# Grouping the score matmuls of an attention job, and sorting the experts ahead of the first expert group

## The chip, the cores and the metric

The kernel runs on 1 core of one Trainium2 chip. The metric is the device time in microseconds (us), the median of 3 runs. A profile of one more execution comes with it: every instruction of the five engines with its start, the DMA queues, and the clock that TensorE was granted (1.00 is 2.4 GHz, 0.50 is 1.2 GHz).

## The reference

One block of a hybrid model on 512 tokens of width 1024. Two branches, differential attention and a chunked state space scan (SSD), are merged through gates and an output projection. Then a hierarchical mixture of experts follows. What the change touches, cut to its core:

```python
# attention: 8 heads, each with two components c of width 64, causal, blocks of 128 queries
scores = einsum('bqhcd,bkhcd->bhcqk', q[:, q_lo:q_hi], k[:, :q_hi]) * scale
probs = softmax(where(causal, scores, -inf), axis=-1)
weights = probs[:, :, 0] - lam * probs[:, :, 1]
outs.append(einsum('bhqk,bkhe->bqhe', weights, v[:, :q_hi]))

# experts: 8 groups of 8, a token takes the 2 best experts of its best group
eid = g_sel * 8 + top_k(e_logits[g_sel], 2)
hid = silu(x @ w_gate[e]) * (x @ w_up[e])      # 64 experts, hidden width 512
out[token] += weight * (hid @ w_down[e])       # summed over the token's 2 experts
```

Everything is float32.

## The kernel before

**Two parts.** Up to the output projection the work is planned by a small scheduler in the program, `Flow`. Jobs with an engine, a cost, a priority and tokens for the buffers are sorted into one fixed order per engine before anything runs. The big weight matrices are cut into units of 512 columns (`unit`, matmuls on line 243). Each is split into a high and a low part, and each product is three matmuls. These unit matmuls have the lowest priority and fill TensorE between the jobs of the attention and of the SSD scan. The expert part behind it is written out by hand, in a loop over groups of experts.

**A score job (`att`, `sc`, lines 664 to 673).** For a head, a block of 128 queries and a component c there is a job of three matmuls into one PSUM bank. The first, line 669, takes all 128 rows of the array: 64 rows with the high part of the scaled queries and 64 with their low part, against the high part of the keys, which stands there twice (`qa`, `kk`). The second, line 671, takes 64 rows: the high part of the queries against the low part of the keys (`kl`), in rows 0 to 63 for c = 0 and 64 to 127 for c = 1. The third, line 673, adds the causal mask through an identity in bf16. The number of keys is 128, 256, 384 or 512. Behind the job VectorE takes the negative row maximum (line 676), ScalarE the exponential with its row sum (680), VectorE joins both components (685 to 687), TensorE transposes the result (692), ScalarE copies it (696), TensorE multiplies it with the values (701) and VectorE scales (709). PSUM has 5 banks for this side work (`side()`).

**The experts.** All 64 experts are computed, in groups whose tokens fill the 128 columns of the stationary operand: a pair has 64 places for each expert, a four 32. Tokens beyond these places go through a loop at the end, which `overflow_tables` prepares. So the experts with most tokens should stand in pairs. `order_tables` (line 1588) sorts them by their counts and permutes the routing tables `ptab` with it. The first `NS` = 4 experts keep their places, so that their weights can be loaded before anything is known of the counts. For the others the queue on SyncE reads the expert's number from the table `perm` and loads from a dynamic address (`source`, line 1216).

An expert has 6 transfers of 1 MB: 4 of gate and up, 2 of down. They are issued in the order of the groups (`tiles`). 15 buffers hold them. `done` and `fill` issue the next ones as matmuls free buffers; in the queue a transfer whose buffer is not yet free holds up all behind it. In the order before, six pairs come first and 13 fours behind them.

**A group (the loop from line 1763).** Gate and up product (`gate_up`, matmuls on line 1701, 8 steps over the width, two of which free one buffer of each expert), SiLU on ScalarE and VectorE (1705 to 1707), the hidden rows transposed (`hidden_t`, 1713), the down product (1724), scaled rows (`weighted`), and one group later the sum into the tokens' rows (`combine`, 1740 to 1746). Selection matrices for two groups are made at a time (`onehot`), and one `gather` (1440 and 1441) collects the tokens' rows for both. `group_slots` (1682 to 1690) transposes a selection matrix and takes the routing weights. In the first group the last six steps of the gather stand between the steps of gate-and-up (`pre`); behind gate-and-up come `group_slots`, `order_tables`, `hidden_t`, `overflow_tables`, the second `group_slots` and the down product, in this order on every engine.

Of the kernel before, what the change touches and what calls it, by code (L numbers as in the profile page):

```python
# [13 lines left out]
AF = mybir.ActivationFunctionType  # L14
# [10 lines left out]
class Flow:  # L25
# [32 lines left out]
    def put(self, j):  # L58
        if j["e"] == "N":
            self.zero.append(j)  # L60
        else:
            self.ready[j["e"]].append(j)
# [56 lines left out]
def block_kernel(ctx: ExitStack, tc: tile.TileContext, I, out):  # L119
    nc = tc.nc  # L120
    V, A, G, T = nc.vector, nc.scalar, nc.gpsimd, nc.tensor
# [6 lines left out]
    def side():  # L128
        return sps.tile([128, 512], F32, name="s")
# [12 lines left out]
    J = fl.job  # L142
# [11 lines left out]
    def cv(n):  # L154
        return 0.07 + n * 0.00104
# [105 lines left out]
    ident = cst([128, 128], "ident")  # L261
    V.tensor_scalar(ident, iot, 0.0, None, op0=OP.is_equal)
    identb = cst([128, 128], "identb", BF)
# [3 lines left out]
    maskq = cst([128, 128], "maskq", BF)  # L267
# [94 lines left out]
    j = sqj[0]  # L362
# [204 lines left out]
    def tl(name, shape, bufs, dt=F32):  # L567
        return pools["at"].tile(shape, dt, name=name, bufs=bufs)
# [5 lines left out]
    def ev_qk(p):  # L574
        S_ = {}
# [81 lines left out]
        def att(qb, hh):  # L657
            kl = (qb + 1) * 128
            qs = slice(qb * 128, kl)
            t = {}  # L660
            h = 2 * p + hh
            vc = slice((h % 4) * 128, (h % 4) * 128 + 128)

            def sc(c):
                if c == 0:
                    t["nm"] = tl("nm", [128, 8], 12)
                t["s", c] = side()
                r = slice(64 * c, 64 * c + 64)
                T.matmul(t["s", c][:, :kl], lhsT=S_["qa"][:, c, hh, qs], rhs=S_["kk"][:, c, hh, :kl],
                         start=True, stop=False)  # L670
                T.matmul(t["s", c][:, :kl], lhsT=S_["qa"][r, c, hh, qs], rhs=S_["kl"][r, hh, :kl],
                         start=False, stop=False)
                T.matmul(t["s", c][:, qs], lhsT=identb, rhs=maskq, start=False, stop=True)

            def mx(c):
                V.tensor_reduce(t["nm"][:, c:c + 1], t["s", c][:, :kl], axis=AX.X, op=OP.max, negate=True)

            def ex(c):
                t["p", c] = tl(("p1", "p2")[c], [128, S], (3, 2)[c])
                A.activation(t["p", c][:, :kl], t["s", c][:, :kl], AF.Exp, bias=t["nm"][:, c:c + 1],  # L680
                             accum_out=t["nm"][:, 2 + c:3 + c])

            def un():
                nm, p1, p2 = t["nm"], t["p", 0], t["p", 1]
                V.reciprocal(nm[:, 4:6], nm[:, 2:4])
                V.tensor_scalar(nm[:, 6:7], nm[:, 2:3], nm[:, 5:6], nlam, op0=OP.mult, op1=OP.mult)
                V.scalar_tensor_tensor(p1[:, :kl], p2[:, :kl], nm[:, 6:7], p1[:, :kl], op0=OP.mult, op1=OP.add)

            def tr():
                t["tp"] = side()  # L690
                for kb in range(qb + 1):
                    T.transpose(t["tp"][:, kb * 128:kb * 128 + 128], t["p", 0][:, kb * 128:kb * 128 + 128], ident)

            def ut():
                t["ut"] = tl("ut", [128, NCH, 128], 2)
                A.activation(t["ut"][:, :qb + 1], t["tp"].rearrange("p (b n) -> p b n", b=4)[:, :qb + 1], AF.Copy)

            def av():
                t["av"] = side()
                for kb in range(qb + 1):  # L700
                    T.matmul(t["av"][:, :128], lhsT=t["ut"][:, kb], rhs=vt[p // 2][:, kb, vc],
                             start=(kb == 0), stop=(kb == qb))

            def ev():
                if qb == 0:
                    asb[hh] = tl("asb", [128, NCH, 128], 4)
                    if hh == 0:
                        st[0] = tl("ast", [128, 3, 2, NCH], 2)
                V.tensor_scalar(asb[hh][:, qb], t["av"][:, :128], t["nm"][:, 4:5], None, op0=OP.mult)

            def eq():
                A.activation(t["av"][:, :128], asb[hh][:, qb], AF.Square, accum_out=st[0][:, 0, hh, qb:qb + 1])

            es = []
            for c in range(2):
                j = J("P", 0.06 + max(0.22, kl * 0.00084), lambda c=c: sc(c), list(trj), prio=2.5, acq=["s"])
                scj[p].append(j)
                j = J("V", cv(kl), lambda c=c: mx(c), [j], prio=1.5)
                es.append(J("A", ca(kl), lambda c=c: ex(c), [j], prio=1.5, acq=[("p1", "p2")[c]], rel=["s"]))
            j = J("V", 0.5 + cv(kl), un, es + [lamj], prio=1.5, rel=["p2"])  # L720
            j = J("P", 0.107 * (qb + 1), tr, [j], prio=2.4, acq=["s"])
            j = J("A", ca(kl), ut, [j], prio=1.4, acq=["ut"], rel=["s", "p1"])
            j = J("P", 0.218 * (qb + 1), av, [j] + vj[p // 2], prio=2.3, acq=["s"], rel=["ut"])
            avj[p].append(j)
            j = J("V", 0.27, ev, [j], prio=1.3, acq=["asb"] if qb == 0 else [])
            eqs.append(J("A", 0.23, eq, [j], prio=1.3, rel=["s"]))
            if qb == 3 and hh == 1:
                finish()
# [391 lines left out]
    def mt(tag, shape, name, dt=F32):  # L1120
        if tag is None:
            return pools["mp"].tile(shape, dt, name=name)
        return pools["mp"].tile(shape, dt, name=name, tag=tag, bufs=tags[tag])
# [72 lines left out]

    NS, NW = 4, 12
    groups = ([list(range(i, i + 2)) for i in range(0, NW, 2)] + [list(range(i, i + 4)) for i in range(NW, 64, 4)])  # L1200
    NG = len(groups)
    tiles = []
    for g_ in groups:
# [383 lines left out]

    def order_tables():

        ox = mt("y", [128, 1024], "ox")  # L1590
        key, i64, w1, lt_ = (ox[:, i * E:i * E + E] for i in range(4))
        bd = ox[:, 512:640]
        kc, pc, cc_ = (ox[:, i:i + 1] for i in (640, 641, 642))
        tT = mt("y", [128, 4, 128], "tT")
        V.tensor_scalar(key, R["cnt"], 64.0, None, op0=OP.mult)
        V.tensor_tensor(key, key, iota1, op=OP.subtract)
        V.tensor_scalar(key[:, :NS], iota1[:, :NS], -1.0, 1.0e6, op0=OP.mult, op1=OP.add)
        V.tensor_tensor(i64, ident[:, :E], ident[:, E:], op=OP.add)
        V.tensor_tensor(w1, key, i64, op=OP.mult)
        V.tensor_reduce(kc, w1, axis=AX.X, op=OP.add)  # L1600
        V.tensor_scalar(lt_, key, kc, None, op0=OP.is_gt)
        V.tensor_reduce(pc, lt_, axis=AX.X, op=OP.add)
        V.tensor_scalar(pc, pc, 1.0, None, op0=OP.add)
        V.memset(bd, 0.0)
        for i in range(2):
            r = slice(64 * i, 64 * i + 64)
            V.tensor_scalar(bd[r, 64 * i:64 * i + 64], iota1[r], pc[r], None, op0=OP.is_equal)
        ps = side()
        T.matmul(ps[:1, :E], lhsT=pidx[:E], rhs=bd[:E, :E], start=True, stop=True)
        V.tensor_copy(R["perm"], ps[:1, :E])  # L1610
        V.tensor_tensor(w1, R["cnt"], i64, op=OP.mult)
        V.tensor_reduce(cc_, w1, axis=AX.X, op=OP.add)
        ps = side()
        T.matmul(ps[:, :E], lhsT=cc_[:E].to_broadcast([E, 128]), rhs=bd[:E, :E], start=True, stop=True)
        V.tensor_copy(R["cnt"], ps[:, :E])
        ps = side()
        for i in range(4):
            T.transpose(ps[:, 128 * i:128 * i + 128], ptab[:, i], ident)
        A.activation(tT, ps.rearrange("p (i n) -> p i n", i=4), AF.Copy)
        ps = side()  # L1620
        for i in range(4):
            T.matmul(ps[:, 128 * i:128 * i + 128], lhsT=tT[:, i], rhs=bd, start=True, stop=True)
        A.activation(ptab, ps.rearrange("p (i n) -> p i n", i=4), AF.Copy)

    def overflow_tables():

# [35 lines left out]
    def gather1(P, xt, k):  # L1662
        ps = side()
        gather_mm(P, 256, ps[:, :256], k, range(NCH))
        A.activation(xt[:, k], ps[:, :256], AF.Copy)
# [94 lines left out]

    xt, P = xt[0], R["P0"]
    pend = None
    for gi, g_ in enumerate(groups):
        n = len(g_)
        w = 128 // n
# [5 lines left out]
                fill()  # L1771

        def pre(k):
            if gi == 0 and 1 <= k < 7:
                gather1(P, xt, k + 1)
            elif last and k == 4:
                combine(*pend)

# [8 lines left out]
        hh = gate_up(xt[:, :, o:o + 128], n, w, wk("gu"), done, pre)  # L1787
        if gi == 0:
            ps_ = group_slots(P, 0)
            order_tables()  # L1790
        elif not last:
            combine(*pend)
        if last:
            keep_warm(8)
        ht = hidden_t(hh, 128)
        if gi == 0:
            overflow_tables()
        pt, sl = ps_
        if gi % 2 == 0:
# [172 lines left out]
```

## Time and profile before

| | us |
|---|---|
| runs | 1858.61, 1858.28, 1858.57; median 1858.57 |
| profiled execution, its own time | 1860.44 |
| its span, first to last instruction | 1858.6 |
| TensorE busy | 1636.6 (88%) |
| VectorE busy | 785.3 (42%) |
| ScalarE busy | 416.3 (22%) |
| GpSimd busy | 316.9 (17%) |
| bytes read | 471.56 MB, 255 GB/s over the span |

The engines are called PE (TensorE; PEld its weight loads), DVE (VectorE), ACT (ScalarE), POOL (GpSimd) and SP (SyncE, which issues the transfers). A busy share is an average over stages that have different limits, so the stretches below are cut where the limit changes. The profile's starts of matmuls are measured and their ends modelled: what one costs in a sequence is read from start to start.

### The profile page before, as it was taken

The page shows a single profiled execution, that of the slowest core. Times are in us where ns is not written, and L with a number is a line of the kernel's source. Part 1 is how long each engine was busy: PE and PEld are TensorE (multiplying, and loading weights), DVE is VectorE, ACT ScalarE, POOL GpSimd, SP SyncE. Part 2 cuts the span into 40 slices and gives each one's busy share as a digit, 9 for nine tenths or more (in the row PEclk, how much of TensorE's full clock was granted, in tenths as well). Part 3 has the DMA queues.
Part 4 walks back from the last instruction along what each step waited for, and adds up shares of the span by engine and source line. Part 5 has one row for each costly group of instructions (what it writes and reads, how often), then busy time and mean ns, then how long its engine had stood idle before and what let it go on. Part 6 is the DMA issues. An engine that isn't in the chain of part 4 may idle for free. (4 is left out here: it accounts for less than half of the span.)

```text
span 1858.6 us, 22998 instructions
## 1 busy us (share of the span) xinstructions
PE 1636.6 (88%) x8767; PEld 1004.8 (54%) x8767; DVE 785.3 (42%) x1487; ACT 416.3 (22%) x839; POOL 316.9 (17%) x331
## 2 busy tenths in 40 slices
PE   8999999999999999998899987868768776787675
PEld 6877778878787877887455442323213231232232
DVE  7688842496968775436433321021101210211112
ACT  4355531254444442122111000001001000010001
POOL 5243421154636353101000000000000000000001
PEclk8999999999999999998899998899899989999998
DMA  5311122222221223356699999999999999999995
GB/s 157 101 57 53 51 76 83 91 69 68 69 80 59 78 61 98 91 215 267 238 389 405 419 414 421 420 420 420 421 420 421 420 421 421 420 420 420 421 420 231
DMA packets 81616, 475.19 MB, mean 256 GB/s; under 512 B 10208, under 2 KB 10592, under 8 KB 35808
## 3 DMA queue, kind: packets, MB, share of 16 engines
q1 hardware_dynamic: 81504, 473.70, 64.8%
q8 instruction: 70, 1.15, 0.2%
q14 instruction: 42, 0.34, 0.1%
HBM read 471.56 MB, written 2.10 MB: 255 GB/s over the span
## 5 line engine op out<-in xcount | busy, mean ns | idle before, releaser
L1701 PE MATMUL g<-ew,xt 128*32 128x512 f32 (+1 forms) x1888 | 418.0, 696 | 159.8 <-DMA ew<-in_gu_dram 159.6
L243 PE MATMUL g<-hH,w 128*128 128x512 f32 x1024 | 344.5, 401 | 0.0
L1701 PEld LDWEIGHTS g<-ew,xt 128*32 128x32 f32 (+1 forms) x1888 | 96.7, 128 | 452.4 <-DMA ew<-in_gu_dram 284.6
L1706 DVE SCALAR_TENSOR_TENSOR hh<-hh,g 128x512 f32<-128x512 f32 x19 | 13.1, 688 | 529.4 <-ACT hh L1705 529.4
L243 PEld LDWEIGHTS g<-hH,w 128*128 128x128 f32 x1024 | 192.4, 188 | 43.1 <-issue 5.3
L243 PE MATMUL g<-hL,w 128*128 128x512 f32 x512 | 199.8, 390 | 0.0
L1724 PE MATMUL s<-ew,hT 128*32 128x512 f32 (+1 forms) x976 | 161.8, 614 | 19.3 <-DMA ew<-in_dn_dram 18.6
L1873 POOL TENSOR_TENSOR fst<-fst 128x1 f32<-128x1 f32 x4 | 1.2, 304 | 974.3 <-ACT fo L1866 974.2
L203 DVE TENSOR_TENSOR w<-stg,w 128x1024 fp32r<-128x1024 f32 x108 | 141.9, 1322 | 55.6 <-ACT w L200 31.9
L1705 ACT ACTIVATE hh<-g 128x512 f32<-128x512 f32 x19 | 11.3, 597 | 542.1 <-PE g L1701 542.1
L198 POOL TENSOR_SCALAR w<-stg 128x1024 fp32r<-128x1024 f32 x60 | 69.6, 1161 | 261.1 <-DMA stg<-in_wu_dram 176.7
L1724 PEld LDWEIGHTS s<-ew,hT 128*32 128x32 f32 (+1 forms) x976 | 45.1, 118 | 117.0 <-issue 70.0
L243 PEld LDWEIGHTS g<-hL,w 128*128 128x128 f32 x512 | 96.4, 188 | 17.0
L1746 DVE TENSOR_TENSOR x<-x,s 128x512 f32<-128x512 f32 x152 | 92.4, 679 | 22.9 <-PE s L1741 22.9
L846 DVE SCALAR_TENSOR_TENSOR xb<-u,cw,xb 128x511 f32<-128x511 f32 (+2 forms) x96 | 81.7, 862 | 23.4 <-ACT xb L842 21.7
L1734 DVE SCALAR_TENSOR_TENSOR yl<-s,sl,yh 128x512 fp32r<-128x512 f32 x38 | 28.4, 750 | 149.0 <-ACT yh L1733 147.7
L1701 PE MATMUL g<-stg,xt 128*32 128x512 f32 (+1 forms) x160 | 88.3, 692 | 2.1 <-DMA stg<-in_gu_dram 1.8
L243 PE MATMUL g<-w,hH 128*128 128x512 f32 x256 | 84.3, 410 | 0.0
L1440 PE MATMUL s<-P,h2H 128*128 128x256 f32 (+1 forms) x320 | 78.5, 288 | 2.3 <-DVE P L1429 2.3
L200 ACT ACTIVATE w<-stg 128x1024 fp32r<-128x1024 f32 x60 | 63.2, 1053 | 75.8 <-DMA stg<-in_wu_dram 62.1
L243 PE MATMUL g<-sH,w 128*128 128x512 f32 x256 | 80.2, 394 | 0.0
L1441 PE MATMUL s<-P,h2L 128*128 128x256 f32 (+1 forms) x320 | 76.7, 282 | 0.0
(338 smaller groups left out, 2487.1 us busy)
## 6 DMA issues: line engine op xcount, KB each, us to landing
ew<-in_gu_dram SPq DMA_DIRECT2D x236, 1024.0 KB, 17.4
ew<-in_dn_dram SPq DMA_DIRECT2D x119, 1024.0 KB, 17.8
stg<-in_wu_dram SPq DMA_DIRECT2D x120, 512.0 KB, 3.6
stg<-in_gu_dram SPq DMA_DIRECT2D x40, 512.0 KB, 17.5
stg<-in_dn_dram SPq DMA_DIRECT2D x11, 512.0 KB, 17.6
xT<-in_xT_dram SPq DMA_DIRECT2D x4, 512.0 KB, 6.1
x<-in_xn_dram SPq DMA_DIRECT2D x2, 1024.0 KB, 10.1
out_dram<-fo SPq DMA_DIRECT2D x8, 256.0 KB, 2.1
```

The source lines that it names most:

```text
L198: G.tensor_scalar(c["h"], c["st"], 1.0, 0.0, op0=OP.mult, op1=OP.add)
L200: A.activation(c["h"], c["st"], AF.Copy)
L203: (G if i % 10 == 9 else V).tensor_tensor(c["lo"], c["st"], c["h"].bitcast(F32), op=OP.subtract)
L243: T.matmul(cell[b], lhsT=x, rhs=y, start=first and i == 0, stop=last and i == 2)
L846: V.scalar_tensor_tensor(x()[:, 3 - k:], t["u"][:, :n], w[:, k:k + 1], x()[:, 3 - k:], op0=OP.mult, op1=OP.add)
L1440: T.matmul(o, lhsT=h2(h2H, c)[:, d], rhs=P[:, c], start=(c == 0), stop=False)
L1441: T.matmul(o, lhsT=h2(h2L, c)[:, d], rhs=P[:, c], start=False, stop=(c == NCH - 1))
L1701: T.matmul(o[es_], lhsT=xt[:, k, es_], rhs=gu(e, k)[:, i * 512:i * 512 + 512], start=(k == 0), stop=(k == 7), tile_position=(0, w * e))
L1706: V.scalar_tensor_tensor(hh, hh, 1.0, pg[:W], op0=OP.add, op1=OP.mult)
L1724: T.matmul(ps[i][es_], lhsT=ht[:, k, es_], rhs=dn(e, k)[:, i * 512:i * 512 + 512], start=(k == 0), stop=(k == 3), tile_position=(0, w * e))
L1734: V.scalar_tensor_tensor(yl[:, i], ps[i][:W], sl[:, :1], yh[:, i].bitcast(F32), op0=OP.mult, op1=OP.subtract)
L1746: V.tensor_tensor(o, o, ps, op=OP.add)
```

## The change

Three things, in one diff.

The two components' score jobs of a head and a query block become one job. It takes two PSUM banks at once and issues both 128-row products, then both masks, then both 64-row products.

`order_tables` is called before the loop over the groups. Its VectorE work is issued there, and its products are handed out as functions that `pre` calls before steps 4 (`counts`), 5 (`turn`) and 7 (`put`) of the first group's gate-and-up. Two products that had a bank each now share one. `overflow_tables` moves from the first group to the fourth.

The groups' order becomes: the two pairs of the fixed experts, six fours, the four pairs with the heaviest of the other experts, and the remaining seven fours.

```diff
-            def sc(c):
-                if c == 0:
-                    t["nm"] = tl("nm", [128, 8], 12)
-                t["s", c] = side()
-                r = slice(64 * c, 64 * c + 64)
-                T.matmul(t["s", c][:, :kl], lhsT=S_["qa"][:, c, hh, qs], rhs=S_["kk"][:, c, hh, :kl],
-                         start=True, stop=False)
-                T.matmul(t["s", c][:, :kl], lhsT=S_["qa"][r, c, hh, qs], rhs=S_["kl"][r, hh, :kl],
-                         start=False, stop=False)
-                T.matmul(t["s", c][:, qs], lhsT=identb, rhs=maskq, start=False, stop=True)
+            def sc():
+                t["nm"] = tl("nm", [128, 8], 12)
+                for c in range(2):
+                    t["s", c] = side()
+                    T.matmul(t["s", c][:, :kl], lhsT=S_["qa"][:, c, hh, qs], rhs=S_["kk"][:, c, hh, :kl],
+                             start=True, stop=False)
+                for c in range(2):
+                    T.matmul(t["s", c][:, qs], lhsT=identb, rhs=maskq, start=False, stop=False)
+                for c in range(2):
+                    r = slice(64 * c, 64 * c + 64)
+                    T.matmul(t["s", c][:, :kl], lhsT=S_["qa"][r, c, hh, qs], rhs=S_["kl"][r, hh, :kl],
+                             start=False, stop=True)
...
+            sj = J("P", 0.35 + kl * 0.00126, sc, list(trj), prio=2.5, acq=["s", "s"])
+            scj[p].append(sj)
             for c in range(2):
-                j = J("P", 0.06 + max(0.22, kl * 0.00084), lambda c=c: sc(c), list(trj), prio=2.5, acq=["s"])
-                scj[p].append(j)
-                j = J("V", cv(kl), lambda c=c: mx(c), [j], prio=1.5)
+                j = J("V", cv(kl), lambda c=c: mx(c), [sj], prio=1.5)
...
-    NS, NW = 4, 12
-    groups = ([list(range(i, i + 2)) for i in range(0, NW, 2)] + [list(range(i, i + 4)) for i in range(NW, 64, 4)])
+    NS, NW, NF = 4, 12, 6
+    fours = [list(range(i, i + 4)) for i in range(NW, 64, 4)]
+    pairs = [list(range(i, i + 2)) for i in range(0, NW, 2)]
+    groups = pairs[:NS // 2] + fours[:NF] + pairs[NS // 2:] + fours[NF:]
...
+        def counts():
+            ps = side()
+            T.matmul(ps[:1, :E], lhsT=pidx[:E], rhs=bd[:E, :E], start=True, stop=True)
+            T.matmul(ps[:, E:2 * E], lhsT=cc_[:E].to_broadcast([E, 128]), rhs=bd[:E, :E], start=True, stop=True)
+            V.tensor_copy(R["perm"], ps[:1, :E])
+            V.tensor_copy(R["cnt"], ps[:, E:2 * E])
...
+        return {4: counts, 5: turn, 7: put}
...
+    ordering = order_tables()
...
         def pre(k):
-            if gi == 0 and 1 <= k < 7:
-                gather1(P, xt, k + 1)
+            if gi == 0:
+                if 1 <= k < 7:
+                    gather1(P, xt, k + 1)
+                if k in ordering:
+                    ordering[k]()
...
             ps_ = group_slots(P, 0)
-            order_tables()
...
-        if gi == 0:
+        if gi == 3:
             overflow_tables()
```

In the order of TensorE, one score job with 512 keys, the two components' banks being the first two `s` of each piece. Before:

```order
L669 MATMUL s_1004<-kk_700,qa_695 128x512
L671 MATMUL s_1004<-kl_711,qa_695 128x512
L673 LDWEIGHTS identb_79
L673 MATMUL s_1004<-maskq_83,identb_79 128x128
L669 MATMUL s_1010<-kk_700,qa_695 128x512
L671 MATMUL s_1010<-kl_711,qa_695 128x512
L673 LDWEIGHTS identb_79
L673 MATMUL s_1010<-maskq_83,identb_79 128x128
```

And now:

```order
L668 MATMUL s_983<-kk_700,qa_695 128x512
L668 MATMUL s_985<-kk_700,qa_695 128x512
L671 LDWEIGHTS identb_79
L671 MATMUL s_983<-maskq_83,identb_79 128x128
L671 LDWEIGHTS identb_79
L671 MATMUL s_985<-maskq_83,identb_79 128x128
L674 MATMUL s_983<-kl_711,qa_695 128x512
L674 MATMUL s_985<-kl_711,qa_695 128x512
```

The same matmuls and weight loads; the 64-row ones (`kl`) stand together at the end.

In the order of TensorE, from the end of the first group's gate-and-up (`g<-stg,xt` and `g<-ew,xt`) to its down product (`s<-ew,hT`). Before, where `ox` and `tT` belong to the sort:

```order
L1701 MATMUL g<-ew,xt 64x512
L1682 MATMUL s<-ident,P 128x128 x4
L1687 MATMUL s<-ptab,P 128x2 x4
L1609 MATMUL s<-ox,pidx 1x64
L1614 MATMUL s<-ox 128x64
L1618 MATMUL s<-ident,ptab 128x128 x4
L1622 MATMUL s<-ox,tT 128x128 x4
L1713 MATMUL s<-ident,hh 128x128 x4
L1682 MATMUL s<-ident,P 128x128 x4
L1687 MATMUL s<-ptab,P 128x2 x4
L1724 MATMUL s<-ew,hT 64x512 x16
```

And now, from the step of gate-and-up before which the sort's first products stand:

```order
L1619 MATMUL s<-ox,pidx 1x64
L1620 MATMUL s<-ox 128x64
L1714 MATMUL g<-ew,xt 64x512 x4
...
L1627 MATMUL s<-ident,ptab 128x128 x4
L1714 MATMUL g<-ew,xt 64x512 x4
...
L1633 MATMUL s<-ox,tT 128x128 x4
L1714 MATMUL g<-stg,xt 64x512
...
L1695 MATMUL s<-ident,P 128x128 x4
L1700 MATMUL s<-ptab,P 128x2 x4
L1726 MATMUL s<-ident,hh 128x128 x4
...
L1737 MATMUL s<-ew,hT 64x512 x16
```

The sort's four products stand inside gate-and-up; behind it only slots, the hidden rows' transposes and slots are left before the down product.

In the order of VectorE, behind the routing weights (`ptab<-og,o`). Before:

```order
L1558 TENSOR_TENSOR ptab<-og,o_6973 128x256
L1706 SCALAR_TENSOR_TENSOR hh<-hh,g 128x512
L1707 TENSOR_TENSOR hh<-hh,g 128x512
L1684 CAST pt<-s 128x512
L1690 TENSOR_SCALAR sl<-s 64x1 x2
L1595 TENSOR_SCALAR ox<-cnt 128x64
L1596 TENSOR_TENSOR ox<-ox,iota_93 128x64
```

And now, where the sort has 15 rows from its first (`ox<-cnt`) to the copy of the counts:

```order
L1563 TENSOR_TENSOR ptab<-og,o_6973 128x256
L1601 TENSOR_SCALAR ox<-cnt 128x64
...
L1621 CAST perm<-s 1x64
L1622 COPY cnt<-s 128x64
L1719 SCALAR_TENSOR_TENSOR hh<-hh,g 128x512
L1720 TENSOR_TENSOR hh<-hh,g 128x512
```

The sort stands ahead of the first group's SiLU (`hh`) instead of behind it.

## Rows read from the trace of the kernel before

**Rows 1.** Busy time of each engine by stretches, with granted clock and transfers

```profile
core 0: us, PE busy (x) PEld busy (x) DVE busy (x) ACT busy (x) POOL busy (x), PEclk, DMA share, GB/s
90.00:242.00 152.00, 152.00 (x800) 115.87 (x799) 128.21 (x288) 84.75 (x277) 56.22 (x75) 1.00 0.16 52
242.00:862.00 620.00, 613.93 (x3190) 498.15 (x3189) 378.38 (x637) 210.60 (x355) 211.71 (x203) 1.00 0.30 99
880.00:902.00 22.00, 22.00 (x113) 10.01 (x112) 1.26 (x7) 3.12 (x8) 0.00 (x0) 0.98 0.66 252
902.00:922.00 20.00, 15.16 (x68) 9.88 (x70) 14.55 (x51) 1.79 (x3) 0.00 (x0) 0.66 0.41 151
922.00:960.00 38.00, 38.00 (x212) 20.22 (x210) 17.80 (x34) 6.24 (x10) 0.00 (x0) 1.00 0.92 366
960.00:1100.00 140.00, 138.38 (x773) 66.75 (x769) 40.23 (x75) 15.66 (x25) 0.00 (x0) 1.00 1.01 413
1100.00:1820.00 720.00, 540.38 (x3063) 196.78 (x3066) 116.67 (x232) 43.76 (x71) 0.00 (x0) 0.91 1.02 420
```

**Rows 2.** TensorE's timeline in the attention: start, duration, engine, line, operation

```profile
155.86 0.48 PE L669 MATMUL s<-kk,qa 128*128 128x512 f32 x1
156.27 0.49 PE L671 MATMUL s<-kl,qa 64*128 64x512 f32 x1
156.69 0.23 PE L673 MATMUL s<-maskq,identb 128*128 128x128 bf16 x1
156.73 0.71 PE L243 MATMUL g<-w,hH 128*128 128x512 f32 x2
...
157.51 0.62 PE L243 MATMUL g<-w,hH 128*128 128x512 f32 x2
...
158.21 0.49 PE L692 MATMUL s<-ident,p 128*128 128x128 f32 x3
...
164.79 0.60 PE L603 MATMUL s<-ident,ra 128*128 128x128 f32 x4
165.23 0.60 PE L692 MATMUL s<-ident,p 128*128 128x128 f32 x4
...
169.16 0.30 PE L669 MATMUL s<-kk,qa 128*128 128x128 f32 x1
169.40 0.32 PE L671 MATMUL s<-kl,qa 64*128 64x128 f32 x1
169.66 0.23 PE L673 MATMUL s<-maskq,identb 128*128 128x128 bf16 x1
```

**Rows 3.** What VectorE waited for, 90 to 242: total, times, longest

```profile
DVE kl L636 <- ACT kk L620: 5.9, 7, 1.4
DVE ra L585 <- PE g L243: 4.7, 3, 1.7
DVE nm L676 <- PE s L673: 3.3, 14, 0.4
DVE qa L629 <- ACT kk L620: 2.8, 4, 1.1
```

**Rows 4.** TensorE's timeline from the first group's slots to the second's gate-and-up

```profile
901.93 0.66 PE L1682 MATMUL s<-ident,P 128*128 128x128 f32 x4
...
906.65 0.37 PE L1609 MATMUL s<-ox,pidx 64*1 64x64 f32 x2 [3.28 <-DVE ox L1607]
...
912.18 1.06 PE L1713 MATMUL s<-ident,hh 128*128 128x128 f32 x4
...
915.52 8.55 PE L1724 MATMUL s<-ew,hT 128*64 128x512 f32 x32
923.90 13.90 PE L1701 MATMUL g<-ew,xt 128*64 128x512 f32 x64
```

**Rows 5.** The transfer queue's timeline behind the first group's gate-and-up

```profile
902.44 18.55 SPq L1238 DMA_DIRECT2D ew<-in_dn_dram  x2
```

**Rows 6.** TensorE's timeline, the start of the fourth pair's gate-and-up

```profile
985.07 0.59 PE L1701 MATMUL g<-stg,xt 128*64 128x512 f32 x1
```

More of the change, by code (lines that the diff above doesn't have):

```diff
@@ L1607, in order_tables, with turn, put @@
             V.tensor_scalar(bd[r, 64 * i:64 * i + 64], iota1[r], pc[r], None, op0=OP.is_equal)
-        ps = side()
-        T.matmul(ps[:1, :E], lhsT=pidx[:E], rhs=bd[:E, :E], start=True, stop=True)
-        V.tensor_copy(R["perm"], ps[:1, :E])
         V.tensor_tensor(w1, R["cnt"], i64, op=OP.mult)
         V.tensor_reduce(cc_, w1, axis=AX.X, op=OP.add)
[L1613 to L1623, printed above, removed]
+        def counts():
[4 more added lines that the diff above has]
+            V.tensor_copy(R["cnt"], ps[:, E:2 * E])
+        def turn():
+            ps = side()
+            for i in range(4):
+                T.transpose(ps[:, 128 * i:128 * i + 128], ptab[:, i], ident)
+            A.activation(tT, ps.rearrange("p (i n) -> p i n", i=4), AF.Copy)
+        def put():
+            ps = side()
+            for i in range(4):
+                T.matmul(ps[:, 128 * i:128 * i + 128], lhsT=tT[:, i], rhs=bd, start=True, stop=True)
+            A.activation(ptab, ps.rearrange("p (i n) -> p i n", i=4), AF.Copy)
+        return {4: counts, 5: turn, 7: put}
     def overflow_tables():
```

## The prediction

> **What bounds the kernel now.** I read the busy time by stretches first. The reader is to see two regimes in it [rows 1]. From 90 to 242 us, the attention, TensorE is busy for all 152.00 us and VectorE for 128.21; from 242 to 862 TensorE is busy for 613.93 of 620. So up to the end of the output projection TensorE's own work sets the time, and what it saves anywhere is passed on. From 960 on the transfers set it: 413 GB/s to 1100 and 420 from there to 1820, while TensorE is busy for only 540.38 of 720 us. All 64 experts' weights are read once whatever the order, so there a microsecond in which no bytes flow moves the end by one. Between the regimes, 902 to 922 moved 151 GB/s and 922 to 960 moved 366.
>
> Next I read TensorE's timeline inside the attention [rows 2], for what a score job costs from start to start, and what VectorE waits for there [rows 3]. Then TensorE's timeline where the first expert group passes from its gate-and-up product to its down product [rows 4], and the transfer queue at the same place [rows 5]. The pace of the pairs is the distance of two starts in TensorE's timeline [rows 4, 6].
>
> **Part 1, the scores.** A job's component is now three matmuls: 128 rows (kk), 64 rows (kl), 128 rows (the mask). For 512 keys they start at 155.86, 156.27 and 156.69, and the next work at 156.73: 0.87 us. For 128 keys it is 169.16, 169.40, 169.66 and about 0.04 more: 0.54 [rows 2]. A plain stream of 512-column matmuls starts three in 0.70 (157.51 to 158.21), 0.23 each; four 128-column transposes take 0.44 (164.79 to 165.23), 0.11 each. So 0.41 for a 512-column kk and 0.24 for a 128-column one hold some 0.15 that appears where the kind of matmul changes from 128 rows to 64, and about 0.2 more goes at the change back (0.42 and 0.26). Two components make four changes; the new order (both kk, both masks, both kl) makes two.
>
> The new job by these rows, for 512 keys: two kk 0.46, the first mask 0.06, the second mask with the change behind it 0.24 (as the 128-column kk), the kl with the change back 0.42: 1.18 against 1.74. For 128 keys: 0.22 + 0.06 + 0.24 + 0.26 = 0.78 against 1.08. That saves 0.56 and 0.30; with 256 and 384 keys put on the line between, 0.39 and 0.47. There are 8 heads with one job of each of the four lengths: 8 x 1.72 = 13.8 us.
>
> This counts the two kl as one, beside each other: they use rows 0 to 63 and 64 to 127 of the array. No row of before has two such matmuls in sequence. What it does show is the other direction, the experts' 64-column halves. 64 of them take 13.90 us, 0.217 each [rows 4]. If they stand one behind the other instead, each job pays one more stream, 0.06 to 0.23, 0.145 on the mean, 32 times: 4.6 us, and the saving is 9.2. So the bounds are 9.2 and 13.8, and I take the upper one for TensorE's own work.
> The Trainium skill, TensorEngine Tiling (Array Packing), section Key Properties, says that different tiles of the array can run matmuls in parallel and that a change of the mode drains the engine. By it the sum would be 13.8; without it 9.2. No run here shows the parallel part yet.
>
> How much of this reaches the end is VectorE's to say. It is busy for 128.21 of the 152 us [rows 1]; its waits that TensorE ended are at least 4.7 + 3.3 us, those that ScalarE ended 5.9 + 2.8 [rows 3]. A faster TensorE can take away only the first kind for sure: VectorE then needs 152 - 8.0 = 144. Without ScalarE's either it is 135. TensorE, 13.8 shorter, would need 138. So the two engines, each in a fixed order, would run within a few per cent of each other, and TensorE would now meet waits, for which it has none today (152.00 of 152.00 busy). The bounds are 0 (VectorE gives back everything; below nothing only if the new interleaving adds stalls, some 3 us) and 13.8; the floor by VectorE lies at 8. I take 10.5, between that floor and the whole. The work after the attention keeps its order up to the experts, so it only moves forward. That both components' banks are taken at once delays the first component's maximum by about half a microsecond; that lies beside TensorE's other work.
>
> **Part 2, the sort ahead of the first group.** At 901.93 the first group's gate-and-up is done; its down product starts at 915.52, 13.59 us later. In between TensorE waits 3.28 for VectorE's sort, runs the sort's four products, and its granted clock falls: the mean of 902 to 922 is 0.66 against 0.98 before [rows 1, 4]. The queue stands on one transfer for 18.55 us from 902.44 [rows 5]: it waits for a buffer that this down product frees. It does not wait for the sort itself, since the first 24 transfers go to the four fixed experts.
>
> In the changed order the sort's VectorE work stands behind the routing weights, when VectorE is busy for only 1.26 of 22 us (880 to 902), and its products lie between the steps of gate-and-up. What remains between gate-and-up and down is the first slots (901.93 to 906.65 - 3.28 = 903.37: 1.44 us), and the transposes of the hidden rows and the second slots. These took 912.18 to 915.52, 3.34 us at the lower level of the clock (1.2 of 2.4 GHz), so 1.7 to 3.3; I take 2.5 with the chain through ScalarE and VectorE behind the slots. The gap becomes 4 us: 9.6 less. The sort's own products now take 906.65 to 912.18, 5.53 us with waits of their own; I put them at 2.0 at the full clock, spread over gate-and-up, and subtract them. The down product took 8.38 us (915.52 to 923.90) and would take 32 x 0.217 = 6.95 at the full clock: 1.4 more. Sum: 9.6 - 2.0 + 1.4 = 9.0 us earlier for the buffers. Bounds: 0 if the clock falls in gate-and-up instead and the gap only moves, and the whole loss of the stretch, 20 x (1 - 151/420) = 12.8. I take 8.6, a little under the sum, since the transfers of gate-and-up are freed up to 2 us later.
>
> The overflow tables leave this place too, most of the 14.55 us for which VectorE is busy from 902 to 922 [rows 1], to the fourth group. There the transfers set the pace, TensorE has a quarter of its time free [rows 1], and only the evacuation of that group's down product stands behind them on VectorE: nothing. If that cover were missing it would cost at most those 15 us once.
>
> **Part 3, the order of the groups.** Two pairs take TensorE 923.90 to 985.07 = 61.2 us [rows 4, 6], and their 24 transfers of 1.05 MB take 59.9 at 420 GB/s. So pairs leave the transfers short whenever they come with full buffers: 960 to 1100 lost 140 x (1 - 413/420) = 2.3 us. A four has the same 24 transfers as two pairs and one round of the fixed work. With the fours in front the queue runs ahead, and when the heavy pairs come TensorE falls behind by only 2.5 us in four pairs, which the transfers under way cover. I take the 2.3; bounds 0 and 2.3 + 4.9 (922 to 960 as well, 38 x (1 - 366/420)).
>
> **Sum.** 10.5 + 8.6 + 2.3 = 21.4 us. The profiled execution took 1860.44 us, 1.84 beyond its span of 1858.6; it would take 1839.0. The median of the runs is 1.87 lower, 1858.57: I predict 1837.
>
> **Rivals.**
> - TensorE's saving arrives whole, because VectorE's waits for ScalarE shrink with it: 13.8 + 10.9 = 24.7, and up to 28 if the changes cost more than I took: 1831 to 1834. For it: 135 us of need against 138. Against it: fixed orders on both engines.
> - VectorE gives most of it back: 4 of 13.8 arrive, 1844. For it: 128 of 152 busy. The same time comes out if the two kl stand one behind the other and VectorE is in the way.
> - The expert stage gains only half, because the sort's products wait inside gate-and-up and the clock falls there: 10.5 + 5 = 15.5, 1843. Against it: the sort's first product comes four steps into gate-and-up, long after VectorE's part is done.
> - The change does not do what it says in the scores: the cost sits in each matmul and not in the change of kind. Then only the experts gain: 1848. Against it: the plain streams at 0.23 and 0.11.
> - The other side: the heavy pairs lose their clock. In before they come behind dense work at 1.00; now they come out of fours whose mean is 0.91 [rows 1]. Four pairs need 122.4 us at 1.00 against 119.8 for their transfers, and 15 buffers hold 37 us of transfers. From a clock below 122.4 / 157 = 0.78 on the end moves out. At the 0.66 of the stretch 902 to 922 the pairs would take 185 us, 28 more than the cover: 1837 + 28 = 1865, slower. Against it: at 922 to 1100 dense pairs run at 1.00.
>
> **How the numbers follow.** The forecast, 1833 to 1841, has 0.50; the whole saving 0.17; VectorE giving back 0.14; half the expert gain 0.12; no gain in the scores 0.04; the pairs without their clock 0.03. The range from 1828 to 1848 leaves out the last and the ends of the others. A measurement of this kernel tells no change from about 0.2%, 3.7 us: faster means below 1854.9. Faster 0.95, same 0.02, slower 0.03.
>
> **What would show it.** In the scores: two starts of kl within a few hundredths of a microsecond, a job of 512 keys at about 1.2 us, and new waits of TensorE for VectorE between 90 and 240. At the first group: some 4 us between gate-and-up and down, a granted clock near 1.00 there, the transfers back at full rate 8 to 9 us earlier, counted from the first gate-and-up. After that 420 GB/s without a dip, through the heavy pairs as well. I am wrong if VectorE's waits swallow the scores' saving, or if the heavy pairs let the rate fall.

## The result, and the profile after

| | before | after |
|---|---|---|
| runs, median (lowest to highest) | 1858.59 (1858.28 to 1860.45), 4 runs | 1837.44 (1836.18 to 1837.94), 4 runs |
| profiled execution, its own time | 1860.44 | 1836.18 |
| its span | 1858.6 | 1834.4 |
| first expert group's gate-and-up starts | 879.7 | 867.9 |
| from there to the end | 978.8 | 966.5 |

The ratio is 0.9883, 95% interval 0.9866 to 0.99: 21 us less, between 19 and 25. The prediction was 1837. The two profiles lie 24 us apart, since the profiled execution of before was the slowest of its runs and that of after the fastest. About 12 us of them lie ahead of the expert stage and 12 in it.

The busy time of the changed kernel by stretches, columns as in [rows 1]:

```profile
90.00:230.00 140.00, 138.22 (x792) 109.63 (x790) 124.92 (x279) 82.46 (x274) 61.38 (x73) 1.00 0.17 54
230.00:850.00 620.00, 614.38 (x3186) 498.29 (x3184) 379.94 (x642) 211.67 (x358) 209.70 (x203) 0.99 0.30 98
868.00:890.00 22.00, 22.00 (x122) 11.20 (x124) 4.35 (x23) 3.28 (x9) 0.00 (x0) 1.00 0.64 241
890.00:910.00 20.00, 20.00 (x106) 8.61 (x108) 6.13 (x14) 3.16 (x5) 0.00 (x0) 1.00 0.91 349
930.00:935.00 5.00, 5.00 (x26) 1.72 (x24) 0.00 (x0) 0.00 (x0) 0.00 (x0) 1.00 0.37 107
950.00:1090.00 140.00, 107.83 (x612) 41.14 (x608) 42.24 (x96) 8.61 (x14) 0.00 (x0) 0.90 1.01 420
1260.00:1410.00 150.00, 144.78 (x816) 72.85 (x814) 41.13 (x77) 18.95 (x31) 0.00 (x0) 1.00 1.01 420
1410.00:1790.00 380.00, 288.48 (x1615) 103.68 (x1616) 61.88 (x122) 21.73 (x36) 0.00 (x0) 0.90 1.02 420
```

In the attention TensorE is no longer busy throughout: 138.22 of 140 us. The stretch behind it, 620 us long, is as before. Where 902 to 922 moved 151 GB/s [rows 1], 890 to 910 moves 349 at a clock of 1.00. From 950 on the rate stays at 420, through the heavy pairs too (1260 to 1410), where TensorE is nearly always busy and its clock is 1.00. One dip is left, 107 GB/s at 930 to 935. The overflow tables now keep VectorE busy from 1021 to 1037, inside the stretch at 420 GB/s.

TensorE's timeline of the changed kernel for two score jobs with 512 keys, columns as in [rows 2]; `x2` is both components:

```profile
149.01 0.61 PE L668 MATMUL s<-kk,qa 128*128 128x512 f32 x2
149.47 0.29 PE L671 MATMUL s<-maskq,identb 128*128 128x128 bf16 x2
149.69 0.50 PE L674 MATMUL s<-kl,qa 64*128 64x512 f32 x2
150.12 0.73 PE L668 MATMUL s<-kk,qa 128*128 128x512 f32 x2
150.69 0.28 PE L671 MATMUL s<-maskq,identb 128*128 128x128 bf16 x2
150.91 0.50 PE L674 MATMUL s<-kl,qa 64*128 64x512 f32 x2
151.34 0.74 PE L243 MATMUL g<-w,hH 128*128 128x512 f32 x2
```

From 149.01 to 150.12 a job takes 1.11 us, the next 1.22; before it was twice 0.87 [rows 2]. The two 64-row matmuls together are done in 0.50, as long as a single one had shown (0.49) [rows 2].

The same timeline from the end of the first gate-and-up to the second, which answers to [rows 4]:

```profile
888.80 1.16 PE L1633 MATMUL s<-ox,tT 128*128 128x128 f32 x8
...
891.76 0.66 PE L1695 MATMUL s<-ident,P 128*128 128x128 f32 x4
892.25 0.95 PE L1700 MATMUL s<-ptab,P 128*128 128x2 f32 x8
893.18 0.66 PE L1726 MATMUL s<-ident,hh 128*128 128x128 f32 x4
893.67 0.60 PE L1695 MATMUL s<-ident,P 128*128 128x128 f32 x4
894.11 0.95 PE L1700 MATMUL s<-ptab,P 128*128 128x2 f32 x8
894.99 7.09 PE L1737 MATMUL s<-ew,hT 128*64 128x512 f32 x32
901.91 1.46 PE L1714 MATMUL g<-ew,xt 128*64 128x512 f32 x6
```

The gap is 3.23 us (891.76 to 894.99) instead of 13.59, without a wait, and the down product takes 6.92 instead of 8.38. And the transfer queue, which answers to [rows 5]:

```profile
892.27 6.72 SPq L1243 DMA_DIRECT2D ew<-in_dn_dram  x2
```

It still stands until the down product frees a buffer, but 6.72 us instead of 18.55.

What VectorE and ScalarE waited for in the attention, 88 to 232, which answers to [rows 3]:

```profile
DVE kl L636 <- ACT kk L620: 2.6, 6, 0.4
DVE ra L585 <- PE g L243: 1.7, 3, 0.8
DVE qa L629 <- ACT kk L620: 0.8, 2, 0.6
ACT p L682 <- DVE nm L678: 27.7, 17, 3.4
```

VectorE's waits for ScalarE's `kk` are 3.4 us instead of 8.7, those for the unit matmuls 1.7 instead of 4.7, and the wait of its maximum for the scores (3.3) is no longer listed; some other waits for ScalarE are longer than before. The exponential (`p`) waits 27.7 us for VectorE's maxima (`nm`).

### The profile page after: what moved, and what is told of

Same layout as the page of the kernel before. It is cut to its first block, busy times and chain, and to the rows that moved or that the text cites. A ratio compares the mean times of both kernels' runs of the same rounds, so it can differ in the third digit from the quotient of the medians.

```text
span 1834.4 us, 22989 instructions
## 1 busy us (share of the span) xinstructions
PE 1621.0 (88%) x8767; PEld 995.2 (54%) x8767; DVE 786.0 (43%) x1487; ACT 414.9 (23%) x839; POOL 321.4 (18%) x331
## 5 line engine op out<-in xcount | busy, mean ns | idle before, releaser
L1714 PE MATMUL g<-ew,xt 128*32 128x512 f32 (+1 forms) x1896 | 412.9, 691 | 151.8 <-DMA ew<-in_gu_dram 151.5
L1737 PE MATMUL s<-ew,hT 128*32 128x512 f32 (+1 forms) x968 | 172.3, 653 | 23.0 <-DMA ew<-in_dn_dram 22.1
L1718 ACT ACTIVATE hh<-g 128x512 f32<-128x512 f32 x19 | 11.3, 597 | 524.6 <-PE g L1714 524.6
L1714 PE MATMUL g<-stg,xt 128*32 128x512 f32 (+1 forms) x152 | 81.6, 673 | 1.7 <-DMA stg<-in_gu_dram 1.6
```

The lines of the kernel that those rows point to most:

```text
L1714: T.matmul(o[es_], lhsT=xt[:, k, es_], rhs=gu(e, k)[:, i * 512:i * 512 + 512], start=(k == 0), stop=(k == 7), tile_position=(0, w * e))
L1737: T.matmul(ps[i][es_], lhsT=ht[:, k, es_], rhs=dn(e, k)[:, i * 512:i * 512 + 512], start=(k == 0), stop=(k == 3), tile_position=(0, w * e))
```

## The experiments

Each stands beside runs of the kernel before on the same chip, whose medians were 1858.58, 1858.70 and 1857.56 in the three sets. Two kernels of one set share their chip. Where a version is compared with the changed kernel of the result, which belongs to none of the sets, the gains of both over their own runs of before give the same difference to 0.2 us. The edits are shown cut to their core; `...` and the comments stand for what is left out.

**The scores alone.** On the kernel before, only `sc` and its job:

```diff
-            def sc(c):
+            def sc():          # both kk, both masks, both kl, as in the change
-                j = J("P", 0.06 + max(0.22, kl * 0.00084), lambda c=c: sc(c), ..., acq=["s"])
+            sj = J("P", 0.35 + kl * 0.00126, sc, list(trj), prio=2.5, acq=["s", "s"])
```

> Only the scores' part of the change, on the kernel before. Theory: this part is worth what it showed in the profile of the changed kernel, where the first expert group starts 11.8 us earlier than before, some of it chance of the two executions: 9 to 12 us faster than before, a 512-key job at 1.16 us from start to start. Rival (the gain lies in the expert stage and the scores' saving is swallowed by VectorE): under 5 us.

Measured: 1847.31 (1845.65 to 1850.55), ratio 0.9941 (0.9927 to 0.9954): 11 us faster, between 9 and 14. A job with 512 keys takes 1.17 us on the mean of 8. The wait in the first expert group is as before, here 10 us earlier:

```profile
891.85 0.66 PE L1684 MATMUL s<-ident,P 128*128 128x128 f32 x4
...
896.57 0.37 PE L1611 MATMUL s<-ox,pidx 64*1 64x64 f32 x2 [3.28 <-DVE ox L1609]
...
905.44 8.55 PE L1726 MATMUL s<-ew,hT 128*64 128x512 f32 x32
913.82 0.60 PE L1703 MATMUL g<-ew,xt 128*64 128x512 f32 x2
```

The gap is again 13.59 us, and the down product is slow again. So the scores are worth about 11. The rest of the change does nothing for them: between the same two matmuls of the attention (the table further down) this version saves 10.2 us and the changed kernel 10.4.

**The sort alone.** The changed kernel with the scores and the groups' order of before:

```diff
-            def sc():
+            def sc(c):         # one job for each component, as before
-    groups = pairs[:NS // 2] + fours[:NF] + pairs[NS // 2:] + fours[NF:]
+    groups = ([list(range(i, i + 2)) for i in range(0, NW, 2)] + ...)
```

> Only the early sort, and the overflow tables in the fourth group; scores and order of groups as before. Theory: 8 to 10 us faster than before, a gap of 3 to 4 us between the first gate-and-up and its down product instead of 13.6, and after it the losses of the pairs as before (960 to 1100 at about 413 GB/s). Rival (the groups' order is what pays, since buffers fill again in the pairs and take back what the sort gave): under 5 us.

Measured: 1849.24 (1848.04 to 1851.96), ratio 0.9956 (0.9943 to 0.997): 8 to 9 us faster, between 6 and 11. The gap between the first gate-and-up and its down product is 3.24 us (901.56 to 904.80), as in the changed kernel. From the first gate-and-up to the end it takes 969.7 us against 978.8. In its busy time by stretches the pairs' losses are all there, with TensorE busy throughout up to 960 and nearly so behind it:

```profile
904.00:940.00 36.00, 36.00 (x207) 20.25 (x207) 11.10 (x22) 5.25 (x9) 0.00 (x0) 1.00 0.96 384
940.00:960.00 20.00, 20.00 (x95) 6.63 (x92) 1.78 (x3) 1.97 (x3) 0.00 (x0) 1.00 0.85 337
960.00:1100.00 140.00, 135.81 (x774) 67.27 (x773) 60.24 (x128) 15.59 (x25) 0.00 (x0) 1.00 1.01 414
```

The pairs do not take back what the sort gave. The move of the overflow tables is part of this version and was not run by itself.

**The groups' order alone**, and the changed kernel without it. The first is the kernel before with one statement changed, the second the changed kernel with that statement as before:

```diff
-    groups = ([list(range(i, i + 2)) for i in range(0, NW, 2)] + ...)
+    groups = pairs[:NS // 2] + fours[:NF] + pairs[NS // 2:] + fours[NF:]
```

> Only the new order of the groups; scores and sort as before. Theory: 2 to 3 us faster than before, the rate at 420 GB/s from 960 on. Rival 1: nothing, since the 2.3 us are only measured beside 420. Rival 2: most of the expert stage's 12 us.

> The changed kernel with the order of the groups before: scores and sort alone. Theory: the dips of the pairs come back, 2 to 3 us slower than the changed kernel. Rival: the order of the groups does nothing here either, as when it stood alone on the kernel before: the time of the changed kernel.

> The changed kernel once more, as the partner of the two others on the same chip. Both theories: 1836 to 1838; it also tells how far two executions of one program lie apart ahead of the expert stage.

Measured alone: 1857.89 (1855.04 to 1859.63, 11 runs), ratio 0.9998 (0.9989 to 1.0007): no difference shown, as the first rival had it. Its rate does stay at 420 from 960 on:

```profile
902.00:922.00 20.00, 16.33 (x68) 9.45 (x70) 14.65 (x47) 1.79 (x3) 0.00 (x0) 0.66 0.40 140
922.00:960.00 38.00, 38.00 (x234) 19.86 (x234) 15.64 (x34) 6.22 (x10) 0.00 (x0) 1.00 0.92 377
960.00:1100.00 140.00, 109.59 (x660) 42.35 (x656) 27.67 (x57) 8.73 (x14) 0.00 (x0) 0.93 1.01 420
```

The interval reaches from 2.0 us faster to 1.3 slower, so the 2.3 us forecast for this part lie just outside it. With the other two parts in place they are shown: without the new order 1839.52 (1839.41 to 1839.74), and the changed kernel once more 1837.19 (1836.28 to 1837.70). That is 2.3 us, the ranges apart. The same stretch of the two, first without the new order and then with it:

```profile
950.00:1090.00 140.00, 136.21 (x778) 67.48 (x774) 60.49 (x128) 15.95 (x26) 0.00 (x0) 1.00 1.00 414
```

```profile
950.00:1090.00 140.00, 107.87 (x612) 41.24 (x608) 42.23 (x96) 8.61 (x14) 0.00 (x0) 0.90 1.02 420
```

Executions of one program also differ ahead of the expert stage. Its start was 879.7 in before and 877.2 in the groups alone, whose code up to there is the same; that is as large as this part's worth. Counted from there to the end, in one profile each, the groups alone take 977.6 us against 978.8 in before, 1.3 less; with the other two parts it is 966.5 against 969.8, 3.3 less. Why the order is worth less by itself stays open.

**Both kl in the same rows.** The changed kernel, with component 1 on the rows of component 0; it leaves out the low part of component 1's keys:

```diff
-                    r = slice(64 * c, 64 * c + 64)
+                    r = slice(0, 64)
```

> The changed kernel, with both components' 64-row products in rows 0 to 63 of the array, so that they can't run beside each other (component 1 gets the wrong low part of the keys). Theory: the second starts one stream after the first, 0.06 to 0.23 us, 0.145 on the mean over 32 jobs: 4.6 us of TensorE's own work, more if its weight load can't run ahead, and TensorE has no other slack in the attention, so 3 to 6 us slower than the changed kernel. Rival (VectorE is the bound in the attention): under 1.5 us, with fewer waits of TensorE there.

Measured: 1839.85 (1838.67 to 1840.31), ratio to before 0.99 (0.9884 to 0.9915): 2.4 us slower than the changed kernel of the result, which is between the two expectations. Its timeline for two such jobs:

```profile
150.13 0.61 PE L668 MATMUL s<-kk,qa 128*128 128x512 f32 x2
150.59 0.29 PE L671 MATMUL s<-maskq,identb 128*128 128x128 bf16 x2
150.81 0.73 PE L674 MATMUL s<-kl,qa 64*128 64x512 f32 x2
151.47 0.73 PE L668 MATMUL s<-kk,qa 128*128 128x512 f32 x2
```

The two kl take 0.66 us from start to start instead of 0.43: in the same rows they stand one behind the other, in different rows beside each other. TensorE's own work grows, but it has no wait left in the attention that the profile lists, and only half of the growth reaches the end.

To see where the rest is, I summed TensorE's time from each start to the next, by what was done, between the 151st and the 751st unit matmul (us):

| | before | after | kl in same rows | one maximum |
|---|---|---|---|---|
| kk | 19.6 | 13.5 | 12.2 | 12.2 |
| masks | 2.5 | 6.9 | 6.9 | 6.9 |
| kl | 21.9 | 11.4 | 16.1 | 11.0 |
| unit matmuls | 143.8 | 144.6 | 144.4 | 144.8 |
| all else | 32.6 | 33.6 | 33.2 | 33.6 |
| sum | 220.4 | 210.0 | 212.7 | 208.6 |

The scores' own work without waits went from 44.0 to 30.1 (12.2 + 6.9 + 11.0, the last column, which still holds one wait of 0.3): 13.9. Of these, 1.7 stay in after in the rows of the scores, as waits (13.5 and 11.4 against 12.2 and 11.0). Another 1.8 went to the work between the jobs, 0.8 of it to the unit matmuls and the rest to the values' products and transposes, with one wait of 0.3 among them. 10.4 arrived. The serial kl cost 5.1 of own work (16.1 against 11.0); the waits it took away give part of that back. With the kl one behind the other the scores' own work is 35.2, so the sorting by kind alone saves 8.8 of the 13.9, and the kl beside each other the other 5.1.

**One maximum for both components**, on the changed kernel and, as a control, on the kernel before:

```diff
             def mx(c):
-                V.tensor_reduce(t["nm"][:, c:c + 1], ...)
+                if c == 0:
+                    V.tensor_reduce(t["nm"][:, c:c + 1], ...)
...
-                A.activation(t["p", c][:, :kl], t["s", c][:, :kl], AF.Exp, bias=t["nm"][:, c:c + 1], ...)
+                A.activation(t["p", c][:, :kl], t["s", c][:, :kl], AF.Exp, bias=t["nm"][:, 0:1], ...)
```

> The changed kernel, with the row maximum of component 0 taken for both components (the softmax is the same in exact arithmetic): 32 of 64 maxima of VectorE, about 15 us, are gone, every order is kept. Theory (VectorE is what swallowed 2 to 4 us of TensorE's saving in the attention, where TensorE now waits 2.7 us): 2 to 4 us faster than the changed kernel, no wait of TensorE left between 88 and 230. Rival (the rest was lost in changes of kind elsewhere on TensorE): under 1 us.

> The same single maximum on the kernel before, as a control. Theory: TensorE has no wait there from 90 to 400, so VectorE's lighter work moves nothing: within 1.5 us of before. Rival (a lighter VectorE helps in any case): 2 to 4 us faster.

Measured: 1835.60 (1834.79 to 1836.02) on the changed kernel, 1.8 us faster than it, just under the 2 to 4 expected; 1858.36 on the kernel before, ratio 0.9999 (0.999 to 1.0008), no difference. The busy time of both, the changed kernel first:

```profile
90.00:230.00 140.00, 139.23 (x797) 110.66 (x796) 115.56 (x254) 82.80 (x274) 60.23 (x75) 1.00 0.18 57
```

```profile
90.00:242.00 152.00, 152.00 (x800) 115.83 (x799) 114.50 (x258) 83.77 (x278) 57.28 (x74) 1.00 0.16 50
```

VectorE lost 9 and 14 us of work in these stretches. In before that is worth nothing; in the changed kernel it is worth about what TensorE's waits there came to, 1.7 us, and two waits of 0.3 are left. (The 2.7 us of the expectation were counted up to 400 and hold 1.0 of the scan behind the attention.) What TensorE waited for in the changed kernel from 88 to 260 (total, times, longest):

```profile
PE s L668 <- ACT s L714: 0.6, 1, 0.6
PE s L668 <- ACT p L682: 0.6, 1, 0.6
PE s L694 <- ACT p L682: 0.3, 1, 0.3
PE s L694 <- ACT s L714: 0.2, 1, 0.2
```

All four are ended by ScalarE's last read of a side bank (the exponential, the squares), and what waits is the next work that needs one. So the waits come through the banks; VectorE, whose maximum stands ahead of the exponential, lengthens the time that they are held. Whether the banks run short because a job takes two of them at once, or because TensorE comes back for them sooner, no run separates.

**The gather behind the down product**, on the changed kernel, for the one dip that is left:

```diff
         elif not last:
-            m = P.shape[2]
-            xt = rows(m)
-            gather(P, m, xt)
             ps_ = group_slots(P, gi + 1)
         yps = down(ht, n, w, wk("dn"), done)
         pend = (pt, *weighted(yps, 128, sl))
+        if gi % 2 and not last:
+            m = P.shape[2]
+            xt = rows(m)
+            gather(P, m, xt)
```

> The changed kernel, with the gather of the odd groups moved from ahead of their down product to behind it. Theory: the second pair's down product frees its buffers some 8 us earlier, and the 3.7 us that are lost at 930 to 935 (107 GB/s) go: 3 to 4 us faster than the changed kernel. Rival: the gather that now stands between down and the next gate-and-up delays that one, and the dip comes behind it: no change.

Measured: 1834.52 (1833.31 to 1835.53), ratio to before 0.9875 (0.986 to 0.989), 2.9 us faster than the changed kernel, at the lower edge of what was expected. The dip at 930 to 935 is gone; a smaller one comes behind it, as the rival had it:

```profile
930.00:935.00 5.00, 5.00 (x45) 5.00 (x44) 1.17 (x2) 1.65 (x3) 0.00 (x0) 1.00 1.00 411
935.00:940.00 5.00, 5.00 (x47) 3.07 (x50) 0.00 (x0) 1.20 (x2) 0.00 (x0) 1.00 1.04 426
940.00:950.00 10.00, 10.00 (x100) 3.11 (x96) 0.00 (x0) 0.00 (x0) 0.00 (x0) 1.00 0.94 368
```

It is ahead of both kernels.

**The second head's scores turned round**, alone on the changed kernel and together with the late gather:

```diff
-                for c in range(2):     # kk, masks, kl
+                for f, first in ((kks, True), (kls, False)) if hh == 0 else ((kls, True), (kks, False)):
+                    f(first)           # for the second head kl, kk, masks
```

> The changed kernel, with the order inside the second head's score job turned round (both kl first, then kk and masks), so that the kl of two jobs that stand one behind the other meet: two changes of kind fewer, about 0.35 us, in each of up to 16 neighbours, 5.6 us of TensorE's own work. Theory: VectorE lets half of it through at most: 1 to 3 us faster than the changed kernel, with more waits of TensorE in the attention. Rival (TensorE alone): 4 to 6 us.

> The changed kernel with the late gather and the turned order of the second head's scores together. Theory: the late gather's 2 to 3 us come, the turned order adds 0 to 1: 2 to 4 us faster than the changed kernel, near 1834. Rival (the two effects are chance of single executions): the time of the changed kernel.

Measured: 1836.58 (1835.47 to 1838.39) alone, 0.9 us below the changed kernel with the ranges overlapping; 1834.66 (1833.61 to 1835.79) together, 2.5 us below the changed kernel of the same set (1837.19), with the ranges apart, and level with the late gather alone. So the late gather's gain comes a second time. Inconclusive for the turned order: at best it is worth a microsecond. TensorE's waits in the attention grow with it from 1.7 to 2.9 us.

## Why the prediction was right

**The scores, 13.8 of own work.** Right, and for the reason given: 13.9 without waits. The jobs cost 1.16 us for 512 keys (mean of 8) where 1.18 was worked out. The terms are less exact than their sum: the second mask was put at 0.24 us and takes 0.15, while the first kk behind another job's kl, in 4 of the 8, takes 0.34 and not 0.23. The two misses nearly cancel, which is luck. The open question, whether the two kl run beside each other, is settled: they do, and it is worth 5.1 us of own work (4.6 forecast), of which 2.4 reach the end.

**10.5 of them at the end.** Right in size (10.4 between the unit matmuls, 11 in the time of the scores alone), only partly for the reason. I put the loss of 3.3 to VectorE, which was to set a floor near 144 us for the stretch. There is no such floor: 152 less 10.4 is 141.6. Between the two unit matmuls of the table VectorE is busy for 164.0 of 220.4 us before and for 164.3 of 210.0 after, so it did the same work in the shorter time. In the same stretch its waits of over 0.15 us that TensorE ended fell from 13.9 to 6.5 us, by 7.4, about what the floor allowed; those that ScalarE ended, which the floor held fixed, fell from 34.8 to 31.9 as well. TensorE lost only 1.7 to waits, for banks that ScalarE had still to read. About as much (1.8) went to work between the jobs, which I had not counted at all. That the two add up to the 3.3 is luck. A rival, the whole 13.8, was thus nearer in mechanism than its chance of 0.17 said.

**The sort, 8.6.** The mechanism is as forecast and the term a little too small. The gap fell by 10.4 (9.6 forecast), gate-and-up grew by some 1.7 (2.0), the down product shortened by 1.46 (1.4). The second gate-and-up came 34.0 us behind the first instead of 44.2, 10.2 earlier; the sort alone gave 9.3 of the median. The overflow tables were put at nothing, and nothing of them shows: the rate is 420 where they stand now.

**The groups, 2.3.** As forecast on the changed kernel (2.3), not shown alone (0.7). The 3.7 us at 930 to 935 stayed. The sum had left them out, though the signs spoke of 420 GB/s without a dip. They belong to the second pair's gather, ahead of the first four, as the late gather shows.

**The rival on the other side**, heavy pairs that lose their clock, did not come: TensorE's clock is 1.00 from 1260 to 1410, where it is busy for 144.78 of 150 us.

The parts alone add up to 11.3 + 9.3 + 0.7 = 21.3 in medians, against 21.2 measured for the whole. The scores act on a stretch of their own, and the middle passes their part on unchanged; the sort and the groups' order both act on the expert stage, and the order is worth 0.7 alone and 2.3 beside the others, so the close agreement is partly chance. From the 751st unit matmul to the first gate-and-up it took 601.8 us before and 601.6 after.

## What to carry to other kernels

Read what a small matmul costs from its start to the next start, and compare it with a plain stream of the same width: time that appears only beside a matmul of another kind belongs to the change of kind, and sorting by kind took most of it away here. A serial piece of work just ahead of a stage that the transfers bound costs its whole length, and more where TensorE's clock falls over it; put it between steps that run anyway. If the next engine is nearly as busy, do not book its busy time together with its waits as a floor: here the waits gave way first.

## What the runs showed of the hardware

- Two 64-row matmuls in the two halves of the array's rows run beside each other: 0.43 us for the pair at 512 columns, 0.66 in the same rows.
- The change of kind costs more on the way back than on the way there. In the changed kernel the first mask takes 0.07 us to the next start (median), the second, with the change to 64 rows behind it, 0.15. The kl pair takes 0.43 where a plain 512-column stream takes 0.23. The 512-column kk behind such a pair takes 0.34; but behind a mask or transposes, which have 128 rows as well, a 512-column unit matmul also takes 0.31, so not all of that is the change of kind.
- In before, TensorE's granted clock fell to its lower level near 905 us, while TensorE waited for 3.28 us, and it stayed there through the short dependent products behind the wait. This costs beyond the wait: the down product began at the lower level and took 8.38 us, where the same 32 matmuls take 6.92 in the changed kernel at 1.00. The clock in before:

```profile
905.00:910.00 5.00, 2.10 (x8) 1.29 (x8) 2.82 (x14) 0.34 (x1) 0.00 (x0) 0.50 0.89 347
910.00:915.00 5.00, 4.69 (x22) 4.69 (x23) 2.27 (x12) 1.45 (x3) 0.00 (x0) 0.50 0.01 5
```
